# A second token tile scored by gathered rows in a fused transformer layer: the expert layer's two dense stages and a row gather share one Trainium2 core

## The chip, the cores and the metric

The kernel runs on one core of a Trainium2 chip. The metric is device time in microseconds (us) of one execution. Engines are TensorE (PE; its weight loads are listed as PEld), VectorE (DVE), ScalarE (ACT), GpSimd (POOL) and SyncE (SP), which here only issues DMAs. Each engine executes its instructions in program order.

## What is computed

One layer of a latent-token model in fp32: 512 tokens of width 2048. Nothing in the first part (modulated RMSNorm, a state-space mixer, a pooling mixer, gates and an output projection) is changed. The last part is an expert layer with 16384 single-neuron experts, in which every token picks 128 of them (8 heads, 16 each) by two key tables of 128 keys. Cut to what matters:

```
cand = v1[..., :, None] + v2[..., None, :]          # sums of two top-16 lists per head
top_s, pos = top_k(cand, 16);  eid = i1 * 128 + i2  # 128 expert numbers per token
g = softmax(top_s)                                  # per head
act = gelu(einsum('td,thkd->thk', h, u_tab[eid])) * g
out = einsum('thk,thkd->td', act, v_tab[eid])       # u_tab, v_tab: 16384 x 2048
x = rmsnorm(x + g2 * out, final_w)
```

## The kernel before

The 512 tokens are four tiles of 128. The expert layer is computed in two ways at once. Tiles 1 to 3 (`DT`) are dense: all 16384 experts are scored for all their tokens by matmuls, and experts that a token didn't pick get weight zero. Tile 0 is gathered: for each of its 128 picks per token, one row of `u` and one row of `v` per token is fetched by an indirect DMA (128 rows of 8 KB, 1.05 MB), and VectorE forms the product and the weighted sum.

**Stage U** (`dense_u`). 128 blocks of 128 experts, two weight chunks of 512 KB each (`wload`: `raw` by SP, `whi` a rounded copy by ScalarE, `wlo` the rest by a subtraction on VectorE or GpSimd). Products are taken in three passes (`mm3`: hi x hi, hi x lo, lo x hi), so a block is 48 matmuls of 128 experts by 384 tokens into `psU`. ScalarE applies Gelu (`sev`), and two blocks at a time go to DRAM (`sd`).

**Gates.** `picks` turns the top-16 lists of a tile into expert numbers and softmax weights; `dense_keys` transposes them; `dense_gates` spreads a tile's weights over the experts: four tokens at a time, VectorE builds one-hot tables (`oh`) and `R`, TensorE multiplies them into `psd` in 12 matmuls, ScalarE copies to `ast`, and every 32 tokens 2 MB go to DRAM (`gds`). 32 such groups are a tile.

**Stage V** (`dense_v`). For four blocks at a time (`weights_load`, `weights`), scores `sr` and gates `gr` are read back, multiplied on GpSimd, and split into `ah` (ScalarE) and `al` (VectorE). 256 chunks of `v`, 512 KB each, go through `wload` as before; each feeds 18 matmuls of 512 columns into `psV`. VectorE adds `psV` into the three result tiles. `add_half` and `finish` apply the residual and the last norm.

**The order.** `wload` calls `tick`, which advances lanes: generators stepped a given number of times per chunk (`lane(rate, ...)`). `lane1` holds `prep` (picks, keys, gates), at 1.1 steps per chunk. `lane0` holds `gather_tile`, one pair of rows per step, at 0.29 in stage U and 0.25 in stage V. Rows live in a ring of three buffers (`rowp`). In step k VectorE forms the dot product of u row k with the tile's h2 (line 1096), ScalarE makes the weight, VectorE adds v row k-1 into the result (line 1089), and GpSimd requests v row k and u row k+1 (line 1081). `lo_pool` is the share of chunks whose `wlo` is made by GpSimd (0.5); the rest is VectorE's. GpSimd's instructions stand in the order in which the program issues them; those of the other engines are ordered at build time by priority. `late`, eight blocks before the end of stage U, drains `lane1` and prepares the first weights of stage V.

## Time and profile before

| | us |
|---|---|
| median of 3 runs (3973.70 to 3977.77) | 3974.51 |
| the profiled execution | 3968.97 |
| its span, first to last instruction | 3966.9 |
| TensorE busy | 3750.0 (95%) |
| VectorE busy | 2561.8 (65%) |
| GpSimd busy | 1761.6 (44%) |
| ScalarE busy | 1187.9 (30%) |

954.40 MB are moved by DMA, 241 GB/s over the span. The busy time of an engine includes what an instruction spends held up after its start, so a busy share is not work alone. Durations of matmuls overlap; their spacing is read from their starts. The profile's row of granted clock shows TensorE at its higher level (2.4 GHz) in nearly all of the span.

### The profile page before, as it was taken

Reading aid. Unit: us, or ns where it says so; the run is one execution under the profiler, and the core shown is the slowest. Engines: PE = TensorE matmul, PEld = TensorE weight load, DVE = VectorE, ACT = ScalarE, POOL = GpSimd, SP = SyncE. Lnnn points to the kernel's source line nnn. Section 1 sums busy time; section 2 is a strip of 40 time slices with the busy share of each in tenths; the row PEclk is TensorE's granted clock in tenths of the full one; section 3 lists DMA queues with packets and bytes.
Section 4 is the critical chain, followed back from the end, with each engine's and each line's share of the span. In section 5 each row is a group of like instructions: output and inputs, shape, how many; then the busy total and the mean of one; then the engine's idle time right before and its main releaser. Section 6 shows DMA issues by size and latency. Waiting matters only on the chain. (4 is left out here: it accounts for less than half of the span.)

```text
span 3966.9 us, 49308 instructions
## 1 busy us (share of the span) xinstructions
PE 3750.0 (95%) x18841; PEld 3196.8 (81%) x18841; DVE 2561.8 (65%) x3331; ACT 1187.9 (30%) x1752; POOL 1761.6 (44%) x997
## 2 busy tenths in 40 slices
PE   5999998889899899899999999999999999999997
PEld 3478876667777778799999999989977887788886
DVE  4364379996563368986767767655666666665664
ACT  4223331112222222333333333323332333333332
POOL 0043115552322323354444444446555666576652
PEclk8999999999999999999999999999999999999999
DMA  8635658789875422477877778778887877887773
GB/s 269 207 124 186 206 166 231 227 227 302 235 233 175 138 70 91 136 263 281 290 272 267 288 273 291 256 289 290 312 300 279 316 285 281 287 318 282 282 277 123
DMA packets 456382, 954.40 MB, mean 241 GB/s; under 512 B 104721, under 2 KB 248465, under 8 KB 421073
## 3 DMA queue, kind: packets, MB, share of 16 engines
q1 hardware_dynamic: 380320, 584.58, 45.5%
q0 software_dynamic: 46464, 301.03, 20.4%
q10 hardware_dynamic: 29360, 65.64, 4.5%
q8 instruction: 147, 2.41, 0.2%
q14 instruction: 91, 0.74, 0.1%
HBM read 859.88 MB, written 94.93 MB: 241 GB/s over the span
## 5 line engine op out<-in xcount | busy, mean ns | idle before, releaser
L125 ACT CAST whi<-wraw 128x1024 fp32r<-128x1024 f32 x712 | 747.2, 1051 | 1825.2 <-PE psU L111 542.1
L126 POOL TENSOR_TENSOR wlo<-wraw,whi 128x1024 fp32r<-128x1024 f32 x284 | 773.4, 2724 | 946.8 <-ACT whi L125 714.4
L126 DVE TENSOR_TENSOR wlo<-wraw,whi 128x1024 fp32r<-128x1024 f32 x428 | 595.7, 1392 | 591.9 <-ACT whi L125 341.8
L112 PE MATMUL psU<-h2Th,wlo 128*128 128x384 f32 x2048 | 693.6, 339 | 31.7 <-DVE wlo L126 20.0
L110 PE MATMUL psU<-h2Th,whi 128*128 128x384 f32 x2048 | 700.4, 342 | 6.5 <-ACT whi L125 6.5
L111 PE MATMUL psU<-h2Tl,whi 128*128 128x384 f32 x2048 | 692.5, 338 | 0.0
L111 PE MATMUL psV<-wlo,ah 128*128 128x512 f32 x1536 | 607.7, 396 | 10.0 <-POOL wlo L126 5.0
L112 PE MATMUL psV<-whi,al 128*128 128x512 f32 x1536 | 607.0, 395 | 0.0
L110 PE MATMUL psV<-whi,ah 128*128 128x512 f32 x1536 | 558.0, 396 | 9.5 <-DVE ffn L1233 5.2
L112 PEld LDWEIGHTS psU<-h2Th,wlo 128*128 128x128 f32 x2048 | 387.2, 189 | 35.9 <-issue 14.2
L1096 DVE SCALAR_TENSOR_TENSOR row<-row,h 128x2048 f32<-128x2048 f32 x128 | 340.9, 2663 | 90.2 <-DMA row<-in_u,eid 90.2
L110 PEld LDWEIGHTS psU<-h2Th,whi 128*128 128x128 f32 x2048 | 389.0, 190 | 8.4 <-ACT whi L125 8.1
L111 PEld LDWEIGHTS psU<-h2Tl,whi 128*128 128x128 f32 x2048 | 388.0, 189 | 0.0
L1089 DVE SCALAR_TENSOR_TENSOR ffn<-row,w,ffn 128x2048 f32<-128x2048 f32 x127 | 357.7, 2816 | 13.5 <-DMA row<-in_v,eid 13.5
L111 PEld LDWEIGHTS psV<-wlo,ah 128*128 128x128 f32 x1536 | 290.8, 189 | 80.7 <-POOL wlo L126 8.2
L110 PEld LDWEIGHTS psV<-whi,ah 128*128 128x128 f32 x1536 | 290.9, 189 | 77.4 <-issue 10.3
L112 PEld LDWEIGHTS psV<-whi,al 128*128 128x128 f32 x1536 | 290.3, 189 | 67.6
L1081 POOL DMA_INDIRECT row<-in_u,eid x128 | 206.2, 1611 | 249.7 <-ACT w L1097 76.6
L1144 DVE TENSOR_TENSOR oh<-io,iT 128x512 bf16<-128x512 bf16 x192 | 168.9, 920 | 193.1 <-PE psd L1152 193.0
L1081 POOL DMA_INDIRECT row<-in_v,eid x128 | 241.0, 1883 | 19.1 <-issue 6.6
L819 DVE SCALAR_TENSOR_TENSOR lacc<-lw,sil,lacc 128x512 f32<-128x512 f32 x240 | 213.6, 890 | 52.1 <-DMA lw<-in_w_mod 50.1
L112 PE MATMUL psg<-hhi,wlo 128*128 128x512 f32 x512 | 205.0, 405 | 25.9 <-DVE wlo L126 25.8
(349 smaller groups left out, 5600.4 us busy)
## 6 DMA issues: line engine op xcount, KB each, us to landing
wraw<-in_uT SPq DMA_DIRECT2D x256, 512.0 KB, 5.2
wraw<-in_v SPq DMA_DIRECT2D x256, 512.0 KB, 6.2
lw<-in_w_mod SPq DMA_DIRECT2D x256, 256.0 KB, 4.3
wraw<-in_w_in SPq DMA_DIRECT2D x96, 512.0 KB, 4.8
wmod<-in_w_mod SPq DMA_DIRECT2D x48, 512.0 KB, 5.1
sd<-sev ACTq DMA_DIRECT2D x64, 384.0 KB, 6.0
gds<-ast ACTq DMA_DIRECT2D x12, 2048.0 KB, 8.8
sr<-sd SPq DMA_DIRECT2D x32, 768.0 KB, 7.2
```

What stands on the lines that cost most here:

```text
L110: mm(ps, a.hi, b.hi, start=start, stop=False)
L111: mm(ps, a.hi, b.lo, start=False, stop=False)
L112: mm(ps, a.lo, b.hi, start=False, stop=stop)
L125: nc.scalar.copy(hi, raw)
L126: ins = (eng or nc.vector).tensor_tensor(lo, raw, hi.bitcast(F32), op=OP.subtract)
L819: nc.vector.scalar_tensor_tensor(acc, w, self.sil[:, k, 0:1], acc, op0=OP.mult, op1=OP.add)
L1081: nc.gpsimd.indirect_dma_start(out=r, out_offset=None, in_=I[tab], in_offset=bass.IndirectOffsetOnAxis(ap=eid[:, k:k + 1], axis=0))
L1089: V.scalar_tensor_tensor(acc, v, w, acc, op0=OP.mult, op1=OP.add)
L1096: V.scalar_tensor_tensor(u, u, 1.0, h2, op0=OP.mult, op1=OP.mult, accum_out=w[:, 0:1])
L1144: V.tensor_tensor(oh[:, q], self.io4, iT[:, q, ts].unsqueeze(1).broadcast_to([P, P, NT]), op=OP.is_equal)
```

## The change

Tile 1 leaves the matmuls of stage U. Its scores come from gathered rows of `u` (`gather_u`: 128 rows, requested two ahead, a dot product each, then one Gelu over all 128 scores and the product with the softmax weights). What was its softmax weight becomes Gelu times weight, which `dense_gates` then spreads over the experts: its gates already hold the finished activations. In stage V it stays dense. Stage U has 256 tokens per matmul instead of 384, `sd` and `sr` are smaller by a third, and `weights` multiplies only tiles 2 and 3, while tile 1's part is split straight from `gr`. Tile 0's whole gather, u rows and v rows, goes to stage V. The rates change, `lo_pool` goes to 0.7 and 0.62, and a third lane spreads tile 1's gates when its last score is done. Lines of the changed kernel are 3 to 33 higher than those of the kernel before.

```diff
+DU = (2, 3)
+UO = len(DT) - len(DU)
+NU = len(DU) * P
...
-            self.h2 = {0: h2p.tile([P, D], F32, name="h2_0")}
+            self.h2 = {0: h2p.tile([P, D], F32, name="h2_0"), 1: tp.tile([P, D], F32, name="h2_1")}
...
+    def row(self, tab, ids, k):
+        r = self.rowp.tile([P, D], F32, tag="row", name=self.nm("row"))
+        self.nc.gpsimd.indirect_dma_start(out=r, out_offset=None, in_=self.I[tab],
+                                          in_offset=bass.IndirectOffsetOnAxis(ap=ids[:, k:k + 1], axis=0))
+        return r
...
+    def gather_u(self, t, res, after):
+
+        nc, V, h2 = self.nc, self.nc.vector, self.h2[t]
+        i1, i2, g = res[t]
+        eid = self.experts(t, res)
+        dots = self.keep.tile([P, NK], F32, name=self.nm("dots"))
+        rows = [self.row("u", eid, k) for k in range(2)]
+        yield
+        for k in range(NK):
+            if k + 2 < NK:
+                rows.append(self.row("u", eid, k + 2))
+            u = rows.pop(0)
+            with self.tc.issue_after(self.last_lo):
+                V.scalar_tensor_tensor(u, u, 1.0, h2, op0=OP.mult, op1=OP.mult, accum_out=dots[:, k:k + 1])
+            yield
+        nc.scalar.activation(dots, dots, AF.Gelu_apprx_tanh)
+        V.tensor_tensor(dots, dots, g, op=OP.mult)
+        res[t] = (i1, i2, dots)
+        after()
...
-    def dense_gates(self, ix):
+    def dense_gates(self, ix, ts):
...
-        for j, t in enumerate(DT):
-            iT, wb = ix[t]
+        for t in ts:
+            j, (iT, wb) = DT.index(t), ix[t]
...
-            ps = self.psA.tile([P, 512], F32, tag="acc", name=self.nm("psU"))[:, 0:ND * P]
+            ps = self.psA.tile([P, 512], F32, tag="acc", name=self.nm("psU"))[:, 0:NU]
...
-                    self.mm3(ps, w[:, kk, :], self.h2T[:, k, DT[0] * P:SEQ], k == 0, k == KT - 1)
+                    self.mm3(ps, w[:, kk, :], self.h2T[:, k, DU[0] * P:SEQ], k == 0, k == KT - 1)
...
-        nc.gpsimd.tensor_tensor(sv, sv, gr, op=OP.mult)
-        self.split(ah, al, sr)
+        no = UO * P // TG
+        nc.gpsimd.tensor_tensor(sv, sv, gr[:, no:], op=OP.mult)
+        first = lambda x: x[:, :, 0:UO * P].rearrange("p i (j t) -> p i j t", t=TG)
+        self.split(first(ah), first(al), gr[:, 0:no].rearrange("p j i t -> p i j t"))
+        self.split(ah[:, :, UO * P:], al[:, :, UO * P:], sr)
...
+            def gated():
+                lane2[2].append(late_gates())
+
+            def late_gates():
+                yield from self.dense_keys(1, res, ix)
+                yield from self.dense_gates(ix, DT[:UO])
+
             def prep():
-                yield from self.picks(self.tkp, 0, res)
-                self.lane0[2].append(self.gather_tile(0, res, acc0))
-                for t in DT:
+                yield from self.picks(self.tkp, 1, res)
+                self.lane0[2].append(self.gather_u(1, res, gated))
+                for t in DU:
                     yield from self.picks(self.tkp, t, res)
                     yield from self.dense_keys(t, res, ix)
+                yield from self.picks(self.tkp, 0, res)
                 self.es_t.close()
                 self.stp = es_u.enter_context(pool(name="ast", bufs=1))
-                yield from self.dense_gates(ix)
-
-            self.lane0 = lane0 = self.lane(0.29, [])
-            lane1 = self.lane(1.1, [prep()])
-            self.lo_acc, self.lo_pool = 0.0, 0.5
+                yield from self.dense_gates(ix, DU)
+
+            self.lane0 = lane0 = self.lane(0.64, [])
+            lane1 = self.lane(1.0, [prep()])
+            lane2 = self.lane(1.6, [])
+            self.lo_acc, self.lo_pool = 0.0, 0.7
...
-                self.drain(lane1)
+                for lane in (lane1, lane0, lane2):
+                    self.drain(lane)
...
-            lane0[0], self.lo_pool = 0.25, 0.5
+            lane0, self.lo_pool = self.lane(0.51, [self.gather_tile(0, res, acc0)]), 0.62
```

GpSimd's order in stage V, before. `row` is a request of a gathered row, `wlo` a subtraction for a chunk of `v`, `sr` the product of scores and gates:

```order
L1081 DMA row_24119<-in_v,eid_12957 128x2048
L1081 DMA row_24121<-in_u,eid_12957 128x2048
L1199 TENSOR_TENSOR sr_24027<-sr_24027,gr_24028 128x12x4x32
L126 TENSOR_TENSOR wlo_24176<-wraw_24174,whi_24175 128x1024
L126 TENSOR_TENSOR wlo_24224<-wraw_24222,whi_24223 128x1024
L1081 DMA row_24233<-in_v,eid_12957 128x2048
L1081 DMA row_24235<-in_u,eid_12957 128x2048
```

And in the changed kernel:

```order
L1075 DMA row_24002<-in_v,eid_23138 128x2048
L1075 DMA row_24004<-in_u,eid_23138 128x2048
L129 TENSOR_TENSOR wlo_24026<-wraw_24024,whi_24025 128x1024
L129 TENSOR_TENSOR wlo_24050<-wraw_24048,whi_24049 128x1024
L1075 DMA row_24059<-in_v,eid_23138 128x2048
L1075 DMA row_24061<-in_u,eid_23138 128x2048
L1230 TENSOR_TENSOR sr_23956<-sr_23956,gr_23957 128x8x4x32
L129 TENSOR_TENSOR wlo_24126<-wraw_24124,whi_24125 128x1024
L1075 DMA row_24135<-in_v,eid_23138 128x2048
```

A pair of requests stands between every one or two subtractions, where it stood after every two; a pair now belongs to two chunks instead of four.

VectorE's order in stage V, before (`row` by `h` is the dot product with tile 0's h2, `ffn` from `row` the weighted add):

```order
L126 TENSOR_TENSOR wlo_24986<-wraw_24984,whi_24985 128x1024
L1089 SCALAR_TENSOR_TENSOR ffn_12575<-row_24905,w_24900,ffn_12575 128x2048
L1096 SCALAR_TENSOR_TENSOR row_24907,w_25014<-row_24907,h_0_10626 128x2048
L126 TENSOR_TENSOR wlo_25047<-wraw_25045,whi_25046 128x1024
L136 TENSOR_TENSOR al_25070<-sr_24927,ah_25069 128x1536
L126 TENSOR_TENSOR wlo_25100<-wraw_25098,whi_25099 128x1024
```

And in the changed kernel:

```order
L1126 SCALAR_TENSOR_TENSOR row_24137,w_24187<-row_24137,h_0_10626 128x2048
L1119 SCALAR_TENSOR_TENSOR ffn_12572<-row_24192,w_24187,ffn_12572 128x2048
L1126 SCALAR_TENSOR_TENSOR row_24194,w_24244<-row_24194,h_0_10626 128x2048
L129 TENSOR_TENSOR wlo_24297<-wraw_24295,whi_24296 128x1024
L1119 SCALAR_TENSOR_TENSOR ffn_12572<-row_24249,w_24244,ffn_12572 128x2048
L1126 SCALAR_TENSOR_TENSOR row_24251,w_24301<-row_24251,h_0_10626 128x2048
```

Products and adds alternate with hardly more than one subtraction between them; an add of pair k stands ahead of the product of pair k+1.

GpSimd's order at the end of stage U, before (`sr` is the product for the first weights of stage V, the `wlo` after it belong to the last blocks of stage U):

```order
L1081 DMA row_22659<-in_u,eid_12957 128x2048
L126 TENSOR_TENSOR wlo_22720<-wraw_22718,whi_22719 128x1024
L1199 TENSOR_TENSOR sr_22759<-sr_22759,gr_22760 128x12x4x32
L126 TENSOR_TENSOR wlo_22805<-wraw_22803,whi_22804 128x1024
L1081 DMA row_22814<-in_v,eid_12957 128x2048
```

And in the changed kernel:

```order
L129 TENSOR_TENSOR wlo_22272<-wraw_22270,whi_22271 128x1024
L1230 TENSOR_TENSOR sr_22548<-sr_22548,gr_22549 128x8x4x32
L129 TENSOR_TENSOR wlo_22566<-wraw_22564,whi_22565 128x1024
L129 TENSOR_TENSOR wlo_22596<-wraw_22594,whi_22595 128x1024
L129 TENSOR_TENSOR wlo_22629<-wraw_22627,whi_22628 128x1024
```

The place of `sr` among the subtractions of stage U's last blocks is nearly the same and the row requests are gone from there; what moved up to it is what it needs: the gates of tile 1, whose last eight `psd` groups now stand directly ahead of these blocks in TensorE's order.

## Rows read from the trace of the kernel before

**Rows 1.** Stretches: us; busy per engine (instructions); clock; DMA share; GB/s.

```profile
0.00:1585.60 1585.60, 1446.26 (x6891) 1123.55 (x6892) 983.34 (x2031) 430.52 (x695) 494.80 (x451) 0.96 0.63 193
1585.60:2850.10 1264.50, 1226.27 (x7343) 1202.30 (x7343) 882.45 (x843) 411.75 (x637) 607.16 (x272) 0.99 0.75 268
2850.10:3943.00 1092.90, 1073.42 (x4594) 867.97 (x4593) 677.53 (x434) 341.42 (x412) 659.66 (x274) 0.99 0.78 280
3943.00:3966.90 23.90, 4.07 (x18) 2.96 (x16) 18.53 (x24) 4.22 (x9) 0.00 (x0) 0.66 0.39 154
```

**Rows 2.** Timeline, PE, both stages: start, us, engine, line, operation, count.

```profile
2101.36 0.34 PE L110 MATMUL psU<-h2Th,whi 128*128 128x384 f32 x1
...
2105.02 0.34 PE L110 MATMUL psU<-h2Th,whi 128*128 128x384 f32 x1
...
2107.65 1.59 PE L1152 MATMUL psd<-R,oh 128*128 128x128 bf16 x12
...
3304.44 0.39 PE L110 MATMUL psV<-whi,ah 128*128 128x512 f32 x1
...
3309.32 0.39 PE L110 MATMUL psV<-whi,ah 128*128 128x512 f32 x1
```

**Rows 3.** Timeline, GpSimd and VectorE, two places in the expert layer.

```profile
3278.41 3.46 POOL L126 TENSOR_TENSOR wlo<-wraw,whi 128x1024 fp32r<-128x1024 f32 x1 [3.82 <-ACT whi L125]
3279.54 4.48 DVE L1096 SCALAR_TENSOR_TENSOR row<-row,h 128x2048 f32<-128x2048 f32 x1
3282.03 2.86 POOL L1081 DMA_INDIRECT row<-in_v,eid  x1 [0.15 <-issue]
...
2739.85 0.96 POOL L1081 DMA_INDIRECT row<-in_v,eid  x1
2740.00 2.29 DVE L1096 SCALAR_TENSOR_TENSOR row<-row,h 128x2048 f32<-128x2048 f32 x1 [5.63 <-DMA row<-in_u,eid]
```

**Rows 4.** By tile: count, duration in ns minimum/median/maximum, first and last start.

```profile
L1096 DVE SCALAR_TENSOR_TENSOR row<-row,h x128: 2277/2290/4500, 1660.6 to 3819.7; 128x2048 f32<-128x2048 f32 x128
L1089 DVE SCALAR_TENSOR_TENSOR ffn<-row,w,ffn x127: 2337/2349/4532, 1702.2 to 3832.3; 128x2048 f32<-128x2048 f32 x127
L126 DVE TENSOR_TENSOR wlo<-wraw,whi x129: 1171/1221/6014, 1588.1 to 2846.5; 128x1024 fp32r<-128x1024 f32 x129
L126 POOL TENSOR_TENSOR wlo<-wraw,whi x128: 2355/2413/6053, 1591.2 to 2841.1; 128x1024 fp32r<-128x1024 f32 x128
L1144 DVE TENSOR_TENSOR oh<-io,iT x192: 409/420/3298, 1675.5 to 2593.0; 128x512 bf16<-128x512 bf16 x192
L1146 DVE TENSOR_TENSOR R<-oh,wb x96: 946/957/3702, 1715.0 to 2596.3; 128x1536 bf16<-128x1536 bf16 x96
L136 DVE TENSOR_TENSOR al<-sr,ah x32: 1745/2436/3222, 2785.3 to 3816.2; 128x1536 fp32r<-128x1536 f32 x32
L1199 POOL TENSOR_TENSOR sr<-sr,gr x32: 3479/3518/3692, 2773.8 to 3811.1; 128x1536 f32<-128x1536 f32 x32
```

**Rows 5.** Groups by line: operation, count | busy us, mean ns | idle before.

```profile
L1052 DVE TENSOR_TENSOR oh<-rf,iota 128x2048 f32<-128x2048 f32 x8 | 18.3, 2284 | 0.0
```

**Rows 6.** DMA totals of stage U, of stage V, and one busy stretch of 20 us.

```profile
DMA packets 73213, 338.51 MB, mean 268 GB/s; under 512 B 7648, under 2 KB 12256, under 8 KB 53472
...
DMA packets 103885, 306.22 MB, mean 280 GB/s; under 512 B 7008, under 2 KB 51552, under 8 KB 88928
...
3220.00:3240.00 20.00, 20.00 (x88) 16.26 (x87) 12.41 (x7) 8.51 (x9) 16.98 (x7) 1.00 1.03 391
```

**Rows 7.** DMA issues of stage U: count, size, median us to landing.

```profile
gds<-ast ACTq DMA_DIRECT2D x12, 2048.0 KB, 8.8
...
gr<-gds SPq DMA_DIRECT2D x3, 768.0 KB, 12.4
row<-in_u,eid POOLq DMA_INDIRECT x72, 9.7
```

**Rows 8.** Stretch near the end of stage U, columns as in rows 1.

```profile
2620.00:2640.00 20.00, 14.58 (x67) 13.61 (x66) 10.58 (x4) 3.70 (x6) 9.24 (x4) 0.83 1.05 387
```

More of the change, by code (lines that the diff above doesn't have):

```diff
@@ L1068, in picks, with experts @@
         yield
+    def row(self, tab, ids, k):
[3 more added lines that the diff above has]
+        return r
+    def experts(self, t, res):
+        i1, i2, g = res[t]
+        ef = self.keep.tile([P, NK], F32, name=self.nm("ef"))
+        self.nc.vector.scalar_tensor_tensor(ef, i1, float(P), i2, op0=OP.mult, op1=OP.add)
+        eid = self.keep.tile([P, NK], I32, name=self.nm("eid"))
+        self.nc.vector.tensor_copy(eid, ef)
+        return eid
+    def gather_u(self, t, res, after):
+        nc, V, h2 = self.nc, self.nc.vector, self.h2[t]
+        i1, i2, g = res[t]
+        eid = self.experts(t, res)
[13 more added lines that the diff above has]
+        after()
     def gather_tile(self, t, res, acc):
         nc, I, V, h2 = self.nc, self.I, self.nc.vector, self.h2[t]
-        i1, i2, g = res[t]
-        ef = self.keep.tile([P, NK], F32, name=self.nm("ef"))
-        V.scalar_tensor_tensor(ef, i1, float(P), i2, op0=OP.mult, op1=OP.add)
-        eid = self.keep.tile([P, NK], I32, name=self.nm("eid"))
-        V.tensor_copy(eid, ef)
-        def row(tab, k):
-            r = self.rowp.tile([P, D], F32, tag="row", name=self.nm("row"))
-            nc.gpsimd.indirect_dma_start(out=r, out_offset=None, in_=I[tab],
-                                         in_offset=bass.IndirectOffsetOnAxis(ap=eid[:, k:k + 1], axis=0))
-            return r
+        g = res[t][2]
+        eid = self.experts(t, res)
+        row = lambda tab, k: self.row(tab, eid, k)
         def vacc(k, v, w):
@@ L1186, in weights_load @@
         i2, j2 = slice(x * 4, x * 4 + 4), slice(x * 4 % NC, x * 4 % NC + 4)
[L1187 removed]
+        sr = self.app.tile([P, 4, NU], F32, tag="sr", name=self.nm("sr"))
         gr = self.app.tile([P, ND * P // TG, 4, TG], F32, tag="gr", name=self.nm("gr"))
@@ L1261, in peer @@
         pool = lambda **k: tc.tile_pool(**k)
-        self.Sd = [self.dram.tile([P, NC, ND * P], F32, name=f"sd{c}") for c in range(P // NC)]
+        self.Sd = [self.dram.tile([P, NC, NU], F32, name=f"sd{c}") for c in range(P // NC)]
         self.Gd = self.dram.tile([P, ND * P // TG, P, TG], F32, name="gds")
```

5 lines of the change are left out of this document (2 added, 3 removed).

## The prediction, made before the change was run

> **What bounds the kernel now.** I read the stretches by stage first [rows 1]: everything before the expert layer (1585.6 us), stage U (`dense_u`, 1264.5 us), stage V (`dense_v`, 1092.9 us) and a tail of 23.9 us after the last matmul. In both stages TensorE is busy 97 to 98% of the time at a granted clock of 0.99, so it sets the pace. VectorE shows 70 and 62% there, GpSimd 48 and 60%, the DMA engines 0.75 and 0.78. Those shares look like room, and the question is whether it is room for what the change adds.
>
> TensorE's price per matmul is the spacing of starts, not the duration, since matmuls overlap [rows 2]. In stage U, 21 matmuls of 384 columns start between 2101.36 and 2105.02: 174.3 ns each. In stage V, 21 of 512 columns start between 3304.44 and 3309.32: 232.4 ns. The two stand as 384 to 512, so columns set the spacing. Stage U is then 6144 x 174.3 ns = 1071 us, plus 96 groups of `psd` at 1.59 us = 153 us, which leaves 41 us of its 1264.5 for waits.
>
> The other thing to see is that VectorE and GpSimd keep each other out [rows 3]. A GpSimd subtraction (`wlo`) ran from 3278.41 to 3281.87. A VectorE row product that started at 3279.54 took 4.48 us and ended 2.15 us after the subtraction; its median is 2.29 us [rows 4]. Next GpSimd's row request of 3282.03 took 2.86 us and ended 0.87 us after that product. The reverse doesn't hold: a product that started at 2740.00, inside a request that ran from 2739.85, took its plain 2.29 us. So I count the two-input operations of VectorE and the tensor operations of GpSimd as one queue, and requests as no holder of it. With undisturbed (median) durations [rows 4, 5], stage U holds this queue now for 72 x 2.29 (products) + 71 x 2.35 (weighted adds) + 129 x 1.22 + 128 x 2.41 (`wlo` on VectorE and on GpSimd) + 192 x 0.42 + 96 x 0.96 (`oh`, `R`) + 16 x 2.28 (`picks`) + 3.5 = 1011 us, 80% of the stage. Stage V holds it for 56 x 2.29 + 57 x 2.35 + 127 x 1.22 + 128 x 2.41 + 31 x 1.75 (`al`, its minimum) + 31 x 3.52 (`sr`) = 889 us, 81%.
>
> By the Trainium skill (SBUF — State Buffer, section "SBUF: two separate sides") that queue is a shared port pair, held for a whole instruction by whichever engine starts first. The rows on the subtraction and the product agree. The page also counts any GpSimd operation as a holder; the product inside a request doesn't show that. Were requests holders at 0.96 us each [rows 3], stage V would carry 246 us more after the change, and the forecast would be near 4370 us.
>
> **The change, part by part.** *TensorE in stage U.* 384 columns become 256. In proportion that is 116.2 ns, and 12 `psd` matmuls of 128 columns, a weight load each, that end within 1.59 us [rows 2] show starts at most 133 ns apart. 6144 x 116.2 = 714 us, with `psd` 867 us: 357 us less work. The bounds are 116 ns and no gain (below, a rival). Stage V's matmuls stay.
>
> *The shared queue in stage U.* All 128 products of tile 1 come in (128 x 2.29 = 293 us) and tile 0's 72 products and 71 adds (332 us) go. `wlo` moves to GpSimd from half to 179 of 256 blocks (the order of instructions): 179 x 2.41 + 77 x 1.22 = 526 us, where it was 466, since GpSimd needs twice VectorE's time for one. `oh`, `R` and `picks` stay (209 us), `sr` shrinks by a third. Sum 1030 us, 19 more than now, and above TensorE's 867. So stage U is no longer bound by TensorE but by VectorE and GpSimd together.
>
> *The shared queue in stage V.* All 128 products and 128 adds of tile 0 fall here, in place of 56 and 57: 293 + 301 us. `wlo`: 98 x 1.22 + 158 x 2.41 = 501 us. `al` 32 x 1.75 = 56 us; `sr` 32 x 3.52 x 2/3 = 75 us, since its third for tile 1 is no product any more. Sum 1226 us, 337 more than now, and 133 above the whole stage's present length.
>
> *How full that queue can be* is what no row of a long stretch shows. Its ends are 0.81 (today, when TensorE sets the pace) and 1.0. I take 0.92, nearer to full, because it now paces both stages; not 1.0, because both engines run in order. A GpSimd `wlo` stands behind the request of u row k+1, which waits until the add of row k-1 has freed one of three buffers, and the block's matmuls wait for that `wlo`. Stage U: 1030 / 0.92 = 1120 us. Stage V: 1226 / 0.92 = 1332 us.
>
> *The DMAs.* Row traffic goes from 256 to 384 rows of 1.05 MB. Stage V's 306.2 MB [rows 6] become 306.2 + 143 x 1.05 - 7.6 (`sr` smaller) = 449 MB; at the best 20 us of today, 391 GB/s [rows 6], that is 1147 us. Stage U's 338.5 MB become 314, 804 us. Both lie under the queue's 1332 and 1120 us, so I add nothing. The three row buffers allow a request to land in 9.7 us [rows 7] and two operations to follow, two pairs a turn: (9.7 + 2 x (2.29 + 2.35)) / 2 = 9.5 us a pair, 1214 us for 128. That is just under 1332 us and the reason why I don't go above 0.92.
>
> *The turn from U to V.* Tile 1's gates can start only after its last product. In the order, the last eight `psd` groups are issued in one run, and behind them GpSimd's first `sr` waits for `gds` to be written and `gr` to be read back, with the `wlo` of stage U's last blocks queued behind it; on VectorE, `al` stands before four more. Nothing covers this: 8.8 + 12.4 us for the two transfers [rows 7], 2.3 for `sr`, 2.4 for `wlo`: 26 us in which TensorE starves. The stretch of 2620 to 2640 us, where it was idle 5.4 us, shows a granted clock of 0.83 [rows 8]; I add 9 us for that restart. 35 us; its ends are 0 (smaller transfers in a quiet moment, other blocks ready) and 50.
>
> *The tail.* Tile 0 is now finished with the others: an add and two scalings more after the last matmul. I take 4 us of the 23.9 us stretch's kind [rows 1], 28 us in all. Keeping h2 of tile 1, one Gelu over its 128 x 128 scores and the split in two halves are single small operations on ScalarE, which is busy a third of either stage [rows 1]; nothing.
>
> *Sum.* 1585.6 + 1120 + 35 + 1332 + 28 = 4101 us, where the span is 3966.9. The profiled run took 3968.97, 2.1 us over its span, and stands 5.5 us under the median of 3974.51. So 4101 + 2.1 + 5.5 = 4109, given as 4110 us: 3.4% slower. What TensorE saves in stage U (357 us) comes out as 110 us, since the shared queue takes over, and stage V gives 239 us back.
>
> **The rivals.** *The queue fills (faster).* Most idle time of VectorE and GpSimd today is waiting for TensorE's pace. If that goes, they may pack without gaps: 1585.6 + 1030 + 35 + 1226 + 28 + 7.6 = 3912 us. It decides from a filling of 0.973 on, since 2256 / 0.973 + 1648.6 is today's span. For it: 20 us stretches exist in which VectorE and GpSimd together show more than 20 us busy (12.4 + 17.0, [rows 6]). Against it: the in-order waits above.
>
> *Another bound (faster).* If the exclusion costs little in the new mix, stage U falls to TensorE's 867 + 41 + 35 us and stage V to the DMAs' 1147 us: 3711 us. By the Trainium skill (HBM Reference, section "Specifications") a core's share is about 358 GB/s, some 425 alone. This trace's 391 GB/s lies between; by the share stage V would be 1253 us and this rival 3817 us. Rows 3 speak against the rival.
>
> *Worse packing (slower still).* If rows, `wlo` and gates lock step, 0.85 gives 4310 us.
>
> *The spacing stays (the gain isn't there).* Weight loads are busy 1202 of stage U's 1264.5 us [rows 1]. If they and not the columns set 174 ns, stage U keeps its 1264.5 + 35 and the whole is 4253 us. Against it: the ratio of the two spacings.
>
> **How the numbers follow.** Forecast, filling 0.88 to 0.972 (3977 to 4220 us): 48%. Filled to the end: 16%. Another bound: 6%. In between, within 0.2%: 6%. Worse packing: 18%. Spacing unchanged: 6%. So faster 22%, same 6%, slower 72%; 0.2% is about what a measurement of this kernel can tell from no change. The range 3900 to 4320 us takes in the filled queue (3912) and a filling down to 0.85 (4310), and leaves out the other bound and the worst packing, some 15%.
>
> **What would show it.** Starts 116 ns apart in stage U, but TensorE busy only 75 to 80% there and in stage V, waiting for `wlo`; long products and adds in stage V (3 us and more); GpSimd's requests waiting for VectorE; DMA share in stage V above today's 0.78; a hole of some 30 us before stage V. It is wrong if stage V ends within 1230 us, or if stage U doesn't fall below 1264 us.

## The result, and the profile after

The changed kernel takes 4197.7 us (median of 4 runs, 4189.62 to 4208.92), the kernel before 3974.1 us beside it: a ratio of 1.0566 with a 95% interval of 1.0533 to 1.0598. The forecast was 4110 us, slower, from a range of 3900 to 4320. The profiled execution has a span of 4187.9 us. By stage, with stage U from its first `psU` matmul to the first `psV` matmul and stage V from there to its last (by this cut the kernel before has 1264.3 and 1096.5 us):

| us | before | forecast | after | off by |
|---|---|---|---|---|
| up to stage U | 1585.9 | 1585.6 | 1591.4 | +6 |
| stage U with the turn | 1264.3 | 1120 + 35 | 1186.2 | +31 |
| stage V | 1096.5 | 1332 | 1383.2 | +51 |
| tail | 20.2 | 28 | 27.1 | -1 |

The stretches of the changed kernel, as [rows 1] has them for before (us; busy time with instructions of TensorE, its weight loads, VectorE, ScalarE, GpSimd; granted clock; DMA share; GB/s):

```profile
0.00:1591.40 1591.40, 1440.62 (x6892) 1118.34 (x6893) 986.05 (x2033) 429.90 (x695) 495.85 (x451) 0.97 0.63 192
1591.40:2777.60 1186.20, 962.24 (x7342) 932.13 (x7341) 850.92 (x838) 369.98 (x497) 733.86 (x308) 0.89 0.75 266
2777.60:4160.80 1383.20, 1162.50 (x4610) 912.60 (x4608) 1036.52 (x645) 371.23 (x581) 946.59 (x447) 0.93 0.89 322
4160.80:4187.90 27.10, 0.40 (x2) 0.00 (x0) 20.96 (x28) 6.86 (x14) 0.00 (x0) 0.56 0.53 193
```

TensorE is busy 81 and 84% where it was 97 and 98%. No engine is full in stage V: VectorE 75%, GpSimd 68%, the DMA engines 0.89. That is the puzzle of this case: a stage that nobody fills and that is 287 us longer.

TensorE itself does what was expected of it. Two of its matmuls in stage U, 27 starts apart, as in [rows 2]:

```profile
2602.17 0.28 PE L113 MATMUL psU<-h2Th,whi 128*128 128x256 f32 x1
...
2605.35 0.28 PE L113 MATMUL psU<-h2Th,whi 128*128 128x256 f32 x1
```

3.18 us for 27 are 117.8 ns each, where 384 columns took 174.3. What it waits for stands in the waits of stage V (engine, line and tile that waited, what it waited for: us in total, times, longest):

```profile
POOL row L1075 <- DVE ffn L1119: 256.6, 93, 6.5
PEld psV L114 <- POOL wlo L129: 224.8, 69, 10.5
...
PE psV L114 <- POOL wlo L129: 195.1, 67, 10.2
```

where TensorE hardly waited for GpSimd in the kernel before:

```profile
PE psV L111 <- POOL wlo L126: 5.0, 6, 1.7
```

The groups of VectorE and GpSimd in stage V of the changed kernel (count, busy us, mean ns, idle before them and what ended it):

```profile
L129 POOL TENSOR_TENSOR wlo<-wraw,whi 128x1024 fp32r<-128x1024 f32 x158 | 414.9, 2633 | 32.6 <-ACT whi L128 30.8
L1126 DVE SCALAR_TENSOR_TENSOR row<-row,h 128x2048 f32<-128x2048 f32 x128 | 381.2, 2978 | 38.8 <-DMA row<-in_u,eid 38.7
L1119 DVE SCALAR_TENSOR_TENSOR ffn<-row,w,ffn 128x2048 f32<-128x2048 f32 x127 | 335.1, 2639 | 100.4 <-DMA row<-in_v,eid 75.6 <-ACT w L1128 21.7 <-ACT whi L128 3.2
L1075 POOL DMA_INDIRECT row<-in_u,eid x128 | 238.7, 1865 | 278.3 <-DVE ffn L1119 256.6 <-DMA wraw<-in_v 11.0 <-issue 6.0
```

A product takes 2.98 us on average against 2.29 undisturbed [rows 4], the request of a `u` row 1.87 against 0.96 [rows 3], and TensorE's largest wait is for a low part (`wlo`) of GpSimd. The long products alone say nothing about the change, though: in stage V of the kernel before they were as long, and the adds longer (3.08 us).

```profile
L1096 DVE SCALAR_TENSOR_TENSOR row<-row,h 128x2048 f32<-128x2048 f32 x57 | 167.8, 2944 | 28.5 <-DMA row<-in_u,eid 28.5
```

What is new is that there are 128 pairs instead of 56, and that TensorE now waits for the two engines. The exclusion of [rows 3] is there in the open, here on VectorE and GpSimd in one place of stage V (start, us, engine, line, operation):

```profile
3400.20 2.28 DVE L1126 SCALAR_TENSOR_TENSOR row<-row,h 128x2048 f32<-128x2048 f32 x1
...
3400.28 3.02 POOL L1075 DMA_INDIRECT row<-in_u,eid  x1 [0.30 <-DVE wlo L129]
...
3424.75 0.95 POOL L1075 DMA_INDIRECT row<-in_u,eid  x1 [5.66 <-DVE ffn L1119]
...
3425.22 6.27 DVE L129 TENSOR_TENSOR wlo<-wraw,whi 128x1024 fp32r<-128x1024 f32 x1 [0.73 <-ACT whi L128]
...
3425.72 2.35 POOL L129 TENSOR_TENSOR wlo<-wraw,whi 128x1024 fp32r<-128x1024 f32 x1
3428.02 2.37 POOL L1230 TENSOR_TENSOR sr<-sr,gr 128x1024 f32<-128x1024 f32 x1
```

The request that begins inside a product ends 0.82 us after it. The VectorE subtraction of 3425.22, 1.22 us long by itself, sits out two GpSimd operations.

### The profile page after: what moved, and what is told of

Same layout as the page of the kernel before. It is cut to its first block, busy times and chain, and to the rows that moved or that the text cites. A ratio compares the mean times of both kernels' runs of the same rounds, so it can differ in the third digit from the quotient of the medians.

```text
span 4187.9 us, 49856 instructions
## 1 busy us (share of the span) xinstructions
PE 3565.7 (85%) x18841; PEld 2963.1 (71%) x18841; DVE 2894.4 (69%) x3541; ACT 1178.0 (28%) x1785; POOL 2176.3 (52%) x1206
## 4 chain that ended last, share of the span: by engine, by line
DMA 16%; PE 14%; POOL 14%; issue 13%; DVE 8%; ACT 1%; POOLq 0%; ACTq 0%; DVEq 0%; SPq 0%
DMA row<-in_v,eid 10%; POOL wlo L129 8%; POOL row L1075 5%; DMA wraw<-in_uT 3%; PE psU L115 2%; DVE row L1101 2%; PE psU L113 2%; PE psU L114 2%; PE psd L1182 2%; DVE oh L1174 1%; PE psq L115 1%; PE psq L113 1%; PE psq L114 1%; DMA row<-in_u,eid 1%; DVE wlo L129 1%
## 5 line engine op out<-in xcount | busy, mean ns | idle before, releaser
L129 POOL TENSOR_TENSOR wlo<-wraw,whi 128x1024 fp32r<-128x1024 f32 x365 | 984.6, 2704 | 467.9 <-ACT whi L128 291.8
L129 DVE TENSOR_TENSOR wlo<-wraw,whi 128x1024 fp32r<-128x1024 f32 x347 | 495.2, 1427 | 536.5 <-ACT whi L128 284.7
L114 PE MATMUL psV<-wlo,ah 128*128 128x512 f32 x1536 | 654.6, 426 | 196.9 <-POOL wlo L129 195.1
L115 PE MATMUL psU<-h2Th,wlo 128*128 128x256 f32 x2048 | 613.5, 301 | 146.0 <-POOL wlo L129 122.2
L1075 POOL DMA_INDIRECT row<-in_u,eid x256 | 468.0, 1828 | 384.0 <-DVE ffn L1119 256.6
L115 PE MATMUL psV<-whi,al 128*128 128x512 f32 x1536 | 642.9, 419 | 0.0
L113 PE MATMUL psU<-h2Th,whi 128*128 128x256 f32 x2048 | 608.8, 298 | 23.6 <-ACT whi L128 23.5
L114 PE MATMUL psU<-h2Tl,whi 128*128 128x256 f32 x2048 | 602.6, 294 | 0.0
L113 PE MATMUL psV<-whi,ah 128*128 128x512 f32 x1536 | 460.8, 398 | 23.8 <-DVE ffn L1266 13.2
L1126 DVE SCALAR_TENSOR_TENSOR row<-row,h 128x2048 f32<-128x2048 f32 x128 | 381.2, 2978 | 38.8 <-DMA row<-in_u,eid 38.7
L1101 DVE SCALAR_TENSOR_TENSOR row<-row,h 128x2048 f32<-128x2048 f32 x128 | 370.6, 2904 | 50.2 <-DMA row<-in_u,eid 50.2
```

Of the source, the lines that this page charges most:

```text
L113: mm(ps, a.hi, b.hi, start=start, stop=False)
L114: mm(ps, a.hi, b.lo, start=False, stop=False)
L115: mm(ps, a.lo, b.hi, start=False, stop=stop)
L129: ins = (eng or nc.vector).tensor_tensor(lo, raw, hi.bitcast(F32), op=OP.subtract)
L1075: self.nc.gpsimd.indirect_dma_start(out=r, out_offset=None, in_=self.I[tab], in_offset=bass.IndirectOffsetOnAxis(ap=ids[:, k:k + 1], axis=0))
L1101: V.scalar_tensor_tensor(u, u, 1.0, h2, op0=OP.mult, op1=OP.mult, accum_out=dots[:, k:k + 1])
```

## The experiments

Each kernel is the changed one with the edit shown, unless said otherwise. Under each stand the stretches of its stages U and V, with the columns of the first block above. Ratios are to the kernel before, with 95% intervals. The stretches come from one profiled execution each. Where a run leaves a stage as it was, stage V took 1383 to 1400 us and stage U 1175 to 1186, so a difference of a stage under some 20 us is no finding.

### What each group of rows costs

**No rows in stage U.** The loop over tile 1's rows only yields:

```
-        rows = [self.row("u", eid, k) for k in range(2)]
...
+        for k in range(NK):
+            yield
```

> The changed kernel without the first-table rows of tile 1 in stage U: its 128 requests and products are left out (its scores are its gates alone); everything else of stage U, its late gates too, and stage V stay. This prices the rows in stage U. Exclusion theory: the sum in U falls by 128 x 2.28 = 292 us to 738, so VectorE and GpSimd stop pacing and TensorE's 867 us of columns is next: U 900 to 960 against 1186, V as it was (1384), the whole 3930 to 3970. DMA theory: 134 MB less of 268, the same fall. If the columns do not come down to 116 ns a matmul (the forecast's own rival), U stays above 1100.

Measured: 3963.6 us, ratio 0.9997 (0.9983 to 1.0011).

```profile
1594.40:2540.60 946.20, 875.07 (x7342) 864.69 (x7342) 493.36 (x581) 370.46 (x496) 446.12 (x180) 0.96 0.57 192
2540.60:3932.90 1392.30, 1163.80 (x4609) 911.79 (x4609) 1029.76 (x644) 371.47 (x580) 945.22 (x447) 0.93 0.88 320
```

Stage U falls to 946 us, TensorE's 867 and 79 more: 318 us less than in the kernel before, so most of what the narrower product saves is there when nothing else is in the way, and the 128 rows of tile 1 cost 240 us.

**No rows in stage V.** `gather_tile` sets its sum to zero and goes straight to the last steps:

```
+        V.memset(acc, 0.0)
-        u, pend = row("u", 0), None
-        yield
-        for k in range(NK):
...
-        vacc(*pend)
```

> The changed kernel without the rows of tile 0 in stage V: its 256 requests, 128 products and 127 additions are left out (its sum is set to zero), the dense part of stage V stays as it is. This prices the whole gather in stage V. Exclusion theory: the sum in V falls from 1226 by 128 x 2.28 + 127 x 2.33 = 588 us to 638; TensorE's 4608 matmuls x 232.4 ns = 1071 us are next, less what no longer pairs: V 1080 to 1110, as long as V of the kernel before, though that one held 56 pairs. If V stayed above 1200, the dense part itself had become slower by the change (the first tile's gates split from their own rows, the larger GpSimd share of low parts).

Measured: 3847.0 us, ratio 0.9709 (0.9693 to 0.9726).

```profile
1605.70:2780.70 1175.00, 958.80 (x7342) 928.38 (x7342) 849.02 (x839) 369.96 (x497) 730.95 (x308) 0.90 0.75 268
2780.70:3831.40 1050.70, 1047.13 (x4610) 865.92 (x4608) 283.28 (x267) 320.11 (x329) 458.12 (x191) 1.00 0.54 170
```

Stage V takes 1051 us at a clock of 1.00, some 20 us under the expected floor of 1071. The dense part lost nothing by the change; the 128 pairs cost 332 us. If the dense part of the kernel before takes as long without rows, which no run shows, its 56 pairs cost 1096.5 - 1050.7 = 46 us: 0.8 us a pair then, 2.6 now.

**One part alone: the kernel before with all of tile 0's pairs in stage V.**

```
-                self.lane0[2].append(self.gather_tile(0, res, acc0))
...
-            lane0[0], self.lo_pool = 0.25, 0.5
+            lane0[2], lane0[0], self.lo_pool = [self.gather_tile(0, res, acc0)], 0.51, 0.62
```

> The kernel before with one part of the change alone: all 128 pairs of tile 0 go to stage V (lane 0.51 and the low-part share 0.62 there, as in the changed kernel), nothing is gathered in stage U, whose columns stay 384. This takes the second half of the change apart from the first. Exclusion theory: U is TensorE's alone, 6144 x 174.3 ns x 1.14 = 1224 us or a little less than the 1264 of the kernel before, 1215 to 1245; V carries the changed kernel's sum, 1226, and its time, 1370 to 1400; the whole 4200 to 4260, so the narrower columns of the change with the rows of tile 1 in U are worth 30 to 60 us only. If V came out below 1300, the loss in V would be due to the split of the first tile's gates and not to the rows.

Measured: 4288.7 us, ratio 1.0834 (1.0816 to 1.0852).

```profile
1588.90:2824.70 1235.80, 1217.81 (x7343) 1197.77 (x7342) 514.13 (x629) 383.99 (x495) 320.59 (x129) 0.99 0.46 154
2824.70:4247.00 1422.30, 1181.84 (x4609) 921.92 (x4607) 1063.98 (x615) 366.82 (x550) 1003.04 (x447) 0.92 0.88 318
```

The loss in stage V belongs to this part alone. V is even 39 us longer than in the changed kernel, and I had not expected that: here GpSimd multiplies all 1536 columns of `sr`, 32 x 3.52 / 3 = 38 us more in the shared queue [rows 4], which the expectation left out and which would account for it; no run takes it out by itself. The other part, tile 1 scored by rows, is worth 4289 - 4198 = 91 us, or 106 by the two ratios.

**One part undone: 384 columns again in stage U.**

```
-            ps = ... name=self.nm("psU"))[:, 0:NU]
+            ps = ... name=self.nm("psU"))[:, 0:ND * P]
-                    self.mm3(ps, w[:, kk, :], self.h2T[:, k, DU[0] * P:SEQ], k == 0, k == KT - 1)
+                    self.mm3(ps, w[:, kk, :], self.h2T[:, k, DT[0] * P:SEQ], k == 0, k == KT - 1)
```

> The changed kernel with one part undone: TensorE multiplies all 384 columns in stage U again (tile 1's 128 are computed and not used), all else as changed. TensorE has 357 us more in U, 1224 in all, above what U takes now (1186). If VectorE and GpSimd pace U as the exclusion theory has it, TensorE's surplus hides most of the 357: U rises to 1240 to 1330, by 55 to 145 us. If TensorE with its gaps paces U still (the columns never went down in time), U rises by nearly 357 to above 1450. V stays at 1384. The whole 4250 to 4340.

Measured: 4298.1 us, ratio 1.0851 (1.0833 to 1.0869).

```profile
1594.30:2878.00 1283.70, 1226.04 (x7343) 1205.45 (x7342) 820.14 (x838) 371.16 (x497) 679.17 (x308) 0.97 0.69 246
2878.00:4278.40 1400.40, 1166.57 (x4609) 912.88 (x4608) 1028.46 (x646) 370.70 (x581) 966.16 (x447) 0.92 0.88 318
```

Some 350 us more of TensorE work lengthen stage U by 97. So the narrower product is worth 97 us of them in this kernel, near the forecast's 110, because TensorE isn't what paces stage U.

### What paces the stages now

**GpSimd's low parts halved.**

```
-            self.lo_acc, self.lo_pool = 0.0, 0.7
+            self.lo_acc, self.lo_pool = 0.0, 0.35
...
-            lane0, self.lo_pool = self.lane(0.51, [self.gather_tile(0, res, acc0)]), 0.62
+            lane0, self.lo_pool = self.lane(0.51, [self.gather_tile(0, res, acc0)]), 0.31
```

> The changed kernel with the share of low parts that GpSimd computes halved (0.35 for 0.7 in stage U, 0.31 for 0.62 in stage V): some 89 and 79 of them move to VectorE, where one takes 1.22 us for 2.41. Exclusion theory (VectorE's two-input operations and GpSimd's tensor operations take turns, their sum paces both stages): the sum falls by 89 x 1.19 = 106 us in U and by 79 x 1.19 = 94 in V, so at the fillings seen (0.87 and 0.886) U goes from 1186 to 1064 and V from 1384 to 1278, the whole from 4198 to about 3970. Row-ring theory (three row buffers and the landing time of a row pace V) and DMA theory (bytes over a rate that is used up): no change, 4180 to 4215, since neither rows nor bytes change.

Measured: 4074.9 us, ratio 1.026 (1.0227 to 1.0292).

```profile
1600.00:2712.50 1112.50, 932.89 (x7343) 901.29 (x7342) 840.08 (x928) 371.07 (x497) 450.71 (x218) 0.93 0.78 284
2712.50:4050.00 1337.50, 1150.74 (x4609) 908.37 (x4608) 1073.17 (x725) 371.77 (x582) 727.70 (x368) 0.93 0.90 333
```

3% faster with neither a byte nor a row less, as the shared queue has it. (GpSimd alone, which has less to do, would have it too; the next run leaves GpSimd's work as it is.) But U fell by 74 us instead of the expected 122, V by 46 instead of 106.

**Short operations.** Products and additions on half of the columns:

```
-  V.scalar_tensor_tensor(u, u, 1.0, h2, ...)
+  V.scalar_tensor_tensor(u[:, 0:1024], u[:, 0:1024], 1.0, h2[:, 0:1024], ...)
-  V.scalar_tensor_tensor(acc, v, w, acc, ...)
+  V.scalar_tensor_tensor(acc[:, 0:1024], v[:, 0:1024], w, acc[:, 0:1024], ...)
```

> The changed kernel with every row product and row addition on half of its 2048 columns, so part of the scores and sums is left out; rows are fetched whole, so requests and bytes stay. Exclusion theory: the sum falls by 128 x 1.15 = 147 us in U and by 255 x 1.16 = 296 in V; U goes from 1186 to about 1015, V from 1384 to 1150 to 1200 (the DMA floor of 1147 is then next), the whole to about 3830 (3790 to 3900). Row-ring theory: a pair takes (9.7 + 4.6) / 2 = 7.2 us, so V falls as well, to 1150 to 1250, but U stays within 40 us. DMA theory: both stages stay within 30 us, the whole 4140 to 4200.

Measured: 4018.2 us, ratio 1.0136 (1.0103 to 1.017).

```profile
1585.20:2690.90 1105.70, 928.82 (x7342) 898.96 (x7341) 696.64 (x838) 371.36 (x497) 636.29 (x308) 0.93 0.79 285
2690.90:3975.80 1284.90, 1131.73 (x4609) 893.37 (x4609) 733.01 (x646) 360.45 (x581) 795.52 (x447) 0.95 0.93 347
```

U fell by 80 us and V by 98, again about half of what the exclusion theory gave (171 and 184 to 234). In stage V the DMA share rose to 0.93: something else stands close behind.

**Half rows.** The same work on VectorE in two halves, but rows of half the bytes (adds are halved like the products, row numbers doubled):

```
-  indirect_dma_start(out=r, out_offset=None, in_=self.I[tab],
+  indirect_dma_start(out=r[:, 0:1024], out_offset=None, in_=self.I[tab].rearrange("n (h d) -> (n h) d", h=2),
-  V.scalar_tensor_tensor(u, u, 1.0, h2, ...)
+  for q in range(2):
+      V.scalar_tensor_tensor(u[:, 1024:2048], u[:, 0:1024], 1.0, h2[:, q * 1024:q * 1024 + 1024], ...)
```

> The changed kernel with rows of half the bytes: every request fetches 1024 columns, and each product and addition reads them twice in two instructions, so part of the tables is left out; VectorE's time for rows stays (about 5% more). Stage U moves 201 MB instead of 268, stage V 315 instead of 449. DMA theory: V falls towards 315 MB / 391 GB/s = 806 us and meets the exclusion sum only above that, so V goes below 1250 and U below 1130, the whole below 4020. Row-ring theory: the landing shrinks from 9.5 us to perhaps 6.5, a pair to 7.9 us, V to 1200 to 1300, U unchanged. Exclusion theory: sums as before or up to 30 us larger, U and V within 40 us of 1186 and 1384, the whole 4160 to 4240.

Measured: 4046.1 us, ratio 1.0193 (1.0163 to 1.0223).

```profile
1593.80:2697.70 1103.90, 930.04 (x7343) 902.86 (x7342) 960.72 (x1094) 368.15 (x497) 670.49 (x308) 0.92 0.67 225
2697.70:4022.90 1325.20, 1147.71 (x4609) 899.76 (x4608) 1123.08 (x1029) 368.18 (x581) 893.71 (x447) 0.94 0.71 235
```

U fell by 82 us and V by 58, although VectorE works longer. The exclusion theory alone, which gave no change, is refuted by this run, as the DMA theory alone is by the two before it. Bytes and the shared queue both count. (Stage U moved 248 MB here and 315 in the changed kernel; the 201 and 268 MB of the expectation are too low.) Smaller rows also land sooner, and this run doesn't separate that from the bytes; the fourth row buffer below, which leaves every row 5 us more, gained less in stage V, which speaks for the bytes.

**Both cuts at once**, the two edits above with one operation on 1024 columns for each row:

```
+  V.scalar_tensor_tensor(u[:, 0:1024], u[:, 0:1024], 1.0, h2[:, 0:1024], ...)
+  indirect_dma_start(out=r[:, 0:1024], ...)
```

> The changed kernel with both cuts at once: rows of half the bytes, and products and additions on those 1024 columns alone, so half of the scores and sums is left out. Apart, the short operations took 80 us from U and 98 from V, the half rows 82 and 58. If two queues that each have their own limit stand beside each other, so that the later one paces, cutting both gives more than the sum: U below 1186 - 162 = 1024 and V below 1383 - 156 = 1227, towards TensorE's 946 and 1051; the whole below 3880. If both cuts only shorten one loop (a row's landing and its operation follow one another in it), they add up: U 1010 to 1050, V 1210 to 1250, the whole 3860 to 3920. If what is left is the fixed order of GpSimd, they give less than their sum: V above 1250.

Measured: 3816.9 us, ratio 0.9626 (0.9602 to 0.965).

```profile
1600.20:2613.10 1012.90, 894.07 (x7342) 875.79 (x7341) 752.12 (x838) 367.17 (x497) 656.06 (x308) 0.94 0.72 245
2613.10:3789.90 1176.80, 1101.47 (x4610) 876.73 (x4608) 748.43 (x646) 367.42 (x581) 841.85 (x447) 0.98 0.78 264
```

In stage U the two add up (173 us against 162). In stage V they give more than their sum, 206 us against 156: in V each cut alone ran into the other limit.

**GpSimd without low parts.** Its share becomes a plain copy on ScalarE, which is busy 27% of stage V:

```
+            if eng is nc.scalar:
+                nc.scalar.copy(lo, raw)
...
-            return self.nc.gpsimd
+            return self.nc.scalar
```

> The changed kernel with GpSimd's share of the low parts (179 in stage U, 158 in V) made on ScalarE as plain copies of the weights, so that part of the computation (the subtraction in these low parts) is left out; VectorE keeps its 78 and 97 with the subtraction. GpSimd is left with the row requests and the gate products. This takes nearly all tensor operations away from GpSimd without giving VectorE more, so VectorE is free to run: exclusion theory: the sums fall by 179 x 2.41 = 431 us to 599 in U and by 158 x 2.41 = 381 to 845 in V, and neither stage is paced by them: U towards TensorE's 946, 960 to 1010, V 1060 to 1110, the whole 3650 to 3740. Row-loop theory (a buffer's round of request, landing, wait for VectorE and operation, 16.0 us in the changed kernel, times 256 rows over 3 buffers is V): without GpSimd's low parts in front of requests and with operations at 2.3 us a round is still about 1.3 + 9.5 + 2.35 + 0.5 = 13.7 us, so V stays at 1150 to 1200 and only U falls, the whole 3760 to 3880. DMA theory: V above 1250.

Measured: 3867.6 us, ratio 0.9744 (0.9717 to 0.9771).

```profile
1599.30:2619.10 1019.80, 923.63 (x7342) 891.80 (x7340) 627.20 (x837) 532.47 (x676) 199.17 (x132) 0.95 0.83 308
2619.10:3803.70 1184.60, 1109.91 (x4607) 881.94 (x4608) 820.81 (x624) 513.75 (x726) 419.51 (x277) 0.97 0.97 368
3803.70:3872.60 68.90, 0.41 (x2) 0.00 (x0) 53.21 (x49) 15.98 (x31) 14.87 (x10) 0.52 0.61 229
```

This is the clearest run on the exclusion: VectorE's work is nearly the same, and stage V lost 199 us, stage U 166. GpSimd by itself has less to do here as well; that it is the exclusion is seen on VectorE, whose busy time in V falls from 1036.5 to 820.8 us, with the product back to 2.47 us on average. And it shows what stands behind: the DMA engines at a share of 0.97 and 368 GB/s over the whole of stage V. The last five pairs were requested only after the weights were through, which is the long tail: with it, the gain from the start of stage V on is 157 us. GpSimd's requests now wait for a free buffer:

```profile
L1129 DVE SCALAR_TENSOR_TENSOR row<-row,h 128x2048 f32<-128x2048 f32 x122 | 300.8, 2466 | 55.9 <-DMA row<-in_u,eid 55.8
...
L1078 POOL DMA_INDIRECT row<-in_u,eid x123 | 197.6, 1606 | 446.4 <-DVE ffn L1122 425.3 <-DMA wraw<-in_v 15.7 <-DVE ffn L1120 2.4
```

What was expected by the row loop (V 1150 to 1200) is what came, but for the DMAs I had set the mark wrongly: at the 368 GB/s that this run sustains, its 436 MB are 1186 us too. Three buffers and the DMA rate can't be told apart by these times; the share of 0.97 says that the DMA engines had little left.

### What doesn't pace them

**A fourth row buffer in stage V.**

```
+            self.rowp = Turns([self.rowp] * 3 + [es_v.enter_context(pool(name="rows3", bufs=1))])
```

> The changed kernel with a fourth row buffer in stage V (three in stage U as they were; to make room, one tile's expert numbers are worked out in place and the first-table scores reuse a tile). Row-ring theory: a pair of rows takes (9.7 + 2 x 4.64) / 3 = 6.3 us instead of 9.5, the ring stops pacing and V falls from 1384 to 1300 or below, the whole to 4110 or below. Exclusion theory: the sum of 1226 us stays; only its filling can rise a little, V 1355 to 1384, the whole 4170 to 4200. DMA theory: no change within 0.5%.

Measured: 4158.8 us, ratio 1.0476 (1.0446 to 1.0506).

```profile
1596.90:2782.60 1185.70, 960.92 (x7342) 929.80 (x7341) 873.80 (x838) 370.02 (x497) 734.61 (x308) 0.89 0.75 266
2782.60:4143.40 1360.80, 1172.61 (x4609) 912.72 (x4609) 1086.85 (x646) 369.37 (x581) 989.33 (x447) 0.93 0.88 327
```

22 us in stage V: 1.6% for a third more buffers, hardly more than the spread (the medians of the whole are 39 us apart). Where the room went is seen by following each buffer round, requests and operations of stage V paired in their order in the timeline (means over 256 rows, us):

| | request | its end to operation | operation | to the next request | round |
|---|---|---|---|---|---|
| changed kernel, 3 buffers | 1.75 | 9.7 | 2.8 | 1.8 | 16.0 |
| fourth buffer | 1.75 | 12.7 | 2.9 | 3.6 | 21.0 |
| halved low parts, 3 | 1.67 | 10.1 | 2.6 | 1.1 | 15.5 |
| short operations and half rows, 3 | 1.44 | 9.0 | 1.7 | 1.4 | 13.5 |

256 rounds over 3 buffers are 1367 us, and that is stage V. But it is hardly a cause: with a fourth buffer a row simply waits longer at both ends for VectorE and GpSimd. The waits of stage V with the fourth buffer:

```profile
POOL row L1075 <- DVE ffn L1120: 123.1, 38, 5.4
...
PE psV L114 <- POOL wlo L129: 81.9, 40, 5.4
```

GpSimd's requests wait half as long for an add, and TensorE's wait for GpSimd's low parts falls from 195 to 82 us. Yet other waits take their place: TensorE is idle 188 us in stage V, where it was idle 221.

**The two requests of a pair apart**, so that a low part stands between them on GpSimd:

```
             v = row("v", k)
             pend = (k, v, w[:, 2:3])
+            yield
             if k + 1 < NK:
...
-            lane0, ... = self.lane(0.51, ...
+            lane0, ... = self.lane(1.02, ...
```

> The changed kernel with the two row requests of a pair apart in stage V's order: the request for the next first-table row comes a weight tile later than the one for the second-table row (a pair takes two steps of a lane that runs at twice the rate), so that on GpSimd, which keeps the written order, a low part stands between them and does not queue behind a request that waits for its buffer. No work is added or left out. Queue theory (low parts held up behind waiting requests make TensorE wait): TensorE's wait for GpSimd's low parts, 197 us in V, falls below 120 and V from 1383 to 1310 to 1350, the whole 4120 to 4165. Exclusion theory and DMA theory: neither the operations nor the bytes change, so the whole stays within 0.7% of 4198, or rises by up to 30 us since the next row is asked for later.

Measured: 4191.8 us, ratio 1.0562 (1.0533 to 1.0592). No change; stage V 1392.5 us. The wait that I meant to remove is still there, in the waits of stage V:

```profile
PE psV L114 <- POOL wlo L129: 194.7, 80, 6.6
```

195 us in the changed kernel, 195 now. The two requests of a pair no longer stand one behind the other, but GpSimd's requests still wait for their buffers, now mostly each with a low part behind it: 252 us for the adds of VectorE, where it was 257. So the edit did not remove what it was meant to, and the run doesn't test it. The fourth buffer did remove much of it, and gained 22 us.

**A version that does all the work, with what helped.** Halved low parts, a fourth buffer, the requests apart, and `weights(0)` called six passes of stage U (twelve weight tiles) later:

```
             if i2 == P - 8:
                 late()
+            if i2 == P - 2:
+                self.weights(0)
```

> A version of the changed kernel that does the whole computation: low parts halved on GpSimd as in the run that did this alone (-74 us in U, -46 in V), a fourth row buffer in stage V (-22), the two requests of a pair apart (unknown, 0 to -70), and the first sums for stage V taken from six weight tiles later, so that the low parts of stage U's last tiles do not stand behind them on GpSimd (0 to -35 at the turn). If the gains add, 4198 - 142 = 4056, less 0 to 105: 3950 to 4060. By the exclusion theory alone the ring and the step bring nothing beyond the 4075 of the halved low parts. Faster than the kernel before (3972) only if nearly all add.

Measured: 4021.6 us, ratio 1.0142 (1.0117 to 1.0167).

```profile
1593.50:2684.60 1091.10, 943.02 (x7342) 911.14 (x7341) 846.54 (x928) 368.76 (x496) 472.31 (x218) 0.93 0.80 288
2684.60:3987.20 1302.60, 1145.08 (x4609) 894.47 (x4608) 1062.66 (x727) 370.94 (x586) 758.96 (x368) 0.95 0.91 343
```

176 us better than the changed kernel, the gains adding up (U -95, V -81), and still 1.4% slower than the kernel before. No run that does all the work beats that.

## Why the prediction was right, and where it was off

**The shared queue paces (right, shown).** Taking GpSimd's low parts off it gave 199 us in V (157 with the tail) and 166 in U with VectorE's work nearly unchanged. Of TensorE's 357 us 347 were there (117.8 ns a matmul; 946 us for stage U without rows) and came out as 97, forecast 110. One sign that the forecast named shows nothing: products of 3 us in stage V were there before the change too.

**How full it can be (the step that was mis-sized).** I took 0.92. Measured are 1226 / 1383 = 0.886 in stage V, the 51 us. The runs point to the term on the DMAs: I divided 449 MB by the best 20 us of before, 391 GB/s [rows 6], got 1147 us, and put that "under" the queue. Over a whole stage these DMAs sustain 368 GB/s at a share of 0.97 (the run without GpSimd's low parts). That is the most that a stage V of these runs kept up. At that rate the changed kernel's bytes are 1210 us, from this line:

```profile
DMA packets 123812, 445.33 MB, mean 322 GB/s; under 512 B 9216, under 2 KB 53760, under 8 KB 90726
```

So stage V has two limits of one size, 1226 us of shared queue and 1210 us of transfers, and each row passes through both. The runs fit this reading. With the queue cut to 930 us, V stopped at 1285, and 1211 us of transfers are 94% of that. With the transfers cut to 311 MB (845 us at that rate; 941 by the DMA share of 0.71), V stopped at 1325, and the queue, 1268 us with its operations in halves of 1.22 and 1.28 us, is 96% of that. With both cut, 1177, of which TensorE's 1051 are 89%. With halved low parts 1132 and 1210 stand beside 1337. That a limit fills its stage to 94 or 96% when the other one is cut was shown; why two equal ones leave 11% of the stage unfilled was not. Three buffers are not the main reason: a fourth gave back 22 of the 157 us that V stands above the queue.

By the Trainium skill (HBM Reference, section "Specifications") a core's share is about 358 GB/s and a core alone gets some 425. This kernel runs on one core, and the sustained 368 GB/s still lies near the lower of the two. An estimate of stage V's transfers from the share, 445 / 358 = 1243 us, would have warned me that two limits were equal: it stood in the rival and not beside the queue.

**Stage U and the turn.** 31 us over the forecast, in which two misses partly cancel. The turn cost less than the 35 us priced. These are stretches at its end:

```profile
2680.00:2700.00 20.00, 18.00 (x152) 17.41 (x152) 12.40 (x19) 6.52 (x9) 1.09 (x1) 1.00 0.44 171
2700.00:2720.00 20.00, 9.29 (x72) 7.89 (x71) 6.69 (x12) 4.59 (x8) 0.00 (x0) 0.50 0.28 119
2720.00:2740.00 20.00, 8.42 (x49) 8.42 (x50) 6.41 (x3) 2.83 (x4) 10.74 (x4) 0.56 0.88 269
```

and GpSimd's first `sr` in the timeline, with its idle time in brackets:

```profile
2726.44 2.34 POOL L1230 TENSOR_TENSOR sr<-sr,gr 128x1024 f32<-128x1024 f32 x1 [45.35 <-issue]
```

The mechanism fits the one named: GpSimd stands before the first `sr`, 45 us, with the low parts of stage U's last tiles behind it, and TensorE starves. It is idle 22 us of the 40 and runs at half clock. The version with `weights(0)` later is 21 us shorter in stage U than halved low parts alone, so the turn is worth some 20 us, no more than the spread of a stage.

What I didn't price is the start. In the first 200 us VectorE is full (198 of 200) with the picks, the one-hot tiles and the first products together, and TensorE gets through 975 of its 7342 matmuls:

```profile
1591.40:1791.40 200.00, 140.17 (x975) 134.87 (x974) 198.36 (x269) 52.40 (x72) 108.66 (x44) 0.83 0.58 204
1791.40:2777.60 986.20, 822.07 (x6370) 797.26 (x6368) 652.56 (x570) 317.59 (x426) 625.20 (x264) 0.91 0.78 278
```

Afterwards it does 6370 in 986 us; at that rate the 975 would have taken 151 us, so the start costs some 49 us. It is not all new: the kernel before got through 995 in its first 200 us of stage U, which by the same working cost it 33 us. A mean filling of a stage can't see that, the first slice of it can.

**The order on GpSimd (wrong as a reason).** I gave the low part behind a waiting request as the reason not to take 1.0. Setting the requests apart doesn't test it, since they waited as long as before. The fourth buffer does: it took 113 us off TensorE's wait for these low parts, and V fell by 22. That 1.0 was not reached is right, but this wait is not the main reason for it.

**The row buffers.** "9.5 us a pair" left out the request's own 1.75 us and the wait for GpSimd's turn, 1.8 us: the round is 16.0 us and the pair 10.7. A fourth buffer gave 22 us, so this was not the limit that it looks like.

**The rivals.** The filled queue is out (0.886), and so is the unchanged spacing (117.8 ns). Another bound: the DMAs are indeed next, at 1185 us without GpSimd's low parts, not the 1147 given. Worse packing, 0.85, was nearer than I made it: the two stages together, 2256 us of queue, took 2547 without the 22 idle us of the turn, 0.886, near the lower edge of the forecast's band (0.88 to 0.972).

## What to carry to other kernels

Before work is moved into a stage, add up the demand on each thing that is shared there (VectorE with GpSimd as one queue, bytes at the rate that a whole stage sustains and not its best stretch), and look at the second largest sum too: two that were equal made this stage 13 to 14% longer than either. Shares of 48 to 78% on VectorE, GpSimd and the DMA engines said nothing of this, and 56 pairs that cost some 0.8 us each did not mean that 128 would. To find which limit paces, cut one at a time and then both; if both together give clearly more than the sum, there are two.
